# Four edits in one: fold transfers on GpSimd's queue and later in the MLP, transposes of memory values moved behind later work, and the two arms of a branch swapped with a branch hint

## The chip, the cores and the metric

One Trainium2 chip, one of its cores. The kernel is one launch; the time is the device time of that launch in microseconds (us). The kernel before was timed in three runs: 2238.1 us median, 2234.99 to 2240.84.

The engines of a core: TensorE (PE in the profile; PEld are its weight loads, which overlap the matmuls), VectorE (DVE), ScalarE (ACT), GpSimd (POOL) and SyncE (SP). SP computes nothing here; it issues most of the DMA transfers, in the order of its instruction queue. An instruction that waits for a semaphore holds everything behind it on its own engine's queue.

## The reference

One inference step of a two-layer decoder in fp32: width 1024, a prompt of 1024 tokens and 8 decode tokens that go along as 8 extra columns, feed-forward width 4096. Cut to what matters here:

```python
mk, mv = [], []
for l in range(2):
    k, v = split(rmsnorm(mem, norm_mem[l]) @ w_mem_kv[l], 2)      # 256 memory tokens, 4 heads of 64
    mk.append(k); mv.append(v)                                    # both are outputs, too
for l in range(2):
    if l == 1:                                                    # shared keys and values of the B layer
        ks, vs = split(rmsnorm(x, norm_kv) @ w_kv, 2)
    h = rmsnorm(x, norm_mix_pre[l])
    if l == 0:
        q, k, v, r, glr, qm = split(h @ w_in_a[0])                # 384, 384, 768, 768, 16, 256 columns
        g = log_sigmoid(glr @ w_gate_up + b_gate) / 16            # decay gates, per token and key column
        o_main = rmsnorm(gla_recurrence(q, k, v, g)) * silu(r)    # 4 heads, chunk-wise
    else:
        q, qm = split(h @ w_in_b[0])                              # 768, 256 columns
        o_main = sliding_window_attention(q, ks, vs)              # window 128, 12 heads, sinks
    o_mem = softmax(qm @ mk[l].T / 8) @ mv[l]                     # cross-attention into the memory
    x = x + rmsnorm(concat(o_main, o_mem) @ w_out[l])
    x = x + rmsnorm(square(relu(rmsnorm(x) @ w_ffn_up[l])) @ w_ffn_down[l])
```

The norm's gain is part of every `rmsnorm`. The chunk-wise recurrence needs the exponential of sums of gates over a block of 128 tokens, and its inverse. Where all gates are small enough both fit into fp32 at once; where not, the block must be cut into levels.

## The kernel before

**Layout.** Activations lie with the 1024 features over 8 groups of 128 partitions and the tokens along the free dimension, in three chunks of 384, 384 and 264 columns. Every fp32 product is made of three matmuls: operands are cut into a high part (an ACT cast, L152) and a rest (a DVE subtraction, L153), and `proj` (L244 to L246) adds high x high, high x rest and rest x high. Weights come as 128x1024 tiles of 512 KB, which `wload` brings in over SP's queue and cuts.

**Order.** The program is written in Python in one order; a planner reorders the instructions of each engine by priority (program order, unless `high_priority` lifts it) and by its own costs and then fixes one queue for each engine. An instruction can so stand in a queue well before or behind its place in the program, and matmuls of later projections fill the waits of attention.

**Stages of layer 0.** (1) Load of x, its norm and the projections of `qm`. (2) `memkv` (L1063): for both layers four units of 128 columns of the memory keys (m = 0, 1) and values (m = 2, 3), alternating with the projections of q and k (`qk_units`). Each unit is a `proj`, then a DVE multiplication by the norm into `kv` (L1073), one of two places in the tile `vtok`, then stores. For a value unit two PE transposes of `kv` follow (L1081), a DVE copy of them (L1082) and, after the last unit of a layer, a store of both units to DRAM (`mvd`, L1087), from where `load_memkv` reads them back. `gate_inputs` (L1168) then multiplies the gates' low-rank inputs by the norm (L1171, L1172, DVE) and sets a row of ones (L1173, L1174, GpSimd); its last piece lies where `memkv` had its transposed values. (3) `mem_attend_prompt` (L374): eight rounds (four pairs of token blocks, two pairs of heads), each a chain of scores (L384, PE), maximum (L389, DVE), exponentials (L392, ACT), division (L396, DVE), transposes (L403, PE), copy (L405, ACT), product with the values (L411, PE) and copy; with it go the `gates` (L1291) and the rest of the q and k projections. Then the attention of the decode tokens (`mem_dec_steps`, L423), and a reduction of all gates to one flag (L1335). (4) Every engine loads the flag into a register (L1463) and branches on it (L1465). The first arm, for small gates, does `one_factor` per block with the projections of v between; the second does the projections and then `by_levels`. With these inputs the first arm runs. In the program's memory the second arm lies behind it, and the first ends with a jump over it. (5) The recurrence (`gla_block`), the output projection, the MLP.

**The MLP** (`mlp`, L610) multiplies most of the hidden width by a Strassen-Winograd scheme: seven products of half-size blocks in place of eight. Its second half runs 49 *phases* (L927 on): seven products (`ORDER` = 1, 7, 6, 5, 2, 3, 4), each of seven steps jj. A phase is 48 matmuls (L910 to L912) into eight PSUM banks, which are emptied at the end of each product by `evict` (L571 to L585, DVE): product 1 by copies, product 6 (phases 14 to 20) with two additions per bank (L577, L578). For each phase, `load_a` brings 516 KB of activations from DRAM (`ra`, L863), `load_w` for four of the products 512 KB of weights (`wr`, L869), both over SP, and `prep` (L873) combines and cuts them on ACT and DVE (L152, L153, L879 to L887). `ra` has three buffers, and loads stand three phases ahead.

**The fold.** During layer 0's phases the twelve weight tiles of layer 1's projections (four of `w_kv`, eight of `w_in_b`) are multiplied by their norms' gains and written to a DRAM buffer `wfd`, from which layer 1 loads them (L1612). `fold(i)` is three instructions around one buffer `wf`: a load (L236, SP), a multiplication (L237, GpSimd) and a store (L238, SP). Fold i stands behind phase 3i + 2. The buffer's pool is closed behind phase 48, and its memory then belongs to the tiles of the MLP's result, written by L980.

Of the kernel before, what the change touches and what calls it, by code (L numbers as in the profile page):

```python
# [16 lines left out]
P = 128  # L17
# [6 lines left out]
NB = SEQ // P  # L24
MEM = 256
# [22 lines left out]
def hybrid_decoder_step(ctx: ExitStack, tc: tile.TileContext, A, O):  # L48
    nc = tc.nc
# [18 lines left out]
    ident = cp.tile([P, P], F32, tag="ident", name="ident")  # L68
# [21 lines left out]
    def nm(s):  # L90
        uid[0] += 1
        return f"{s}_{uid[0]}"
# [35 lines left out]
    def stps(tag=None):  # L128
        turn[1] ^= 1
        tag = tag or ("sf", "sx")[turn[1]]  # L130
        return pst.tile([P, 512], F32, tag=tag, name=nm(tag))
# [88 lines left out]
    def wstage(src, pool=None):  # L220
        with tc.high_priority(WPRI):
            ws = (pool or wp).tile([P, KT, P], F32, tag="ws", name=nm("ws"))
            nc.sync.dma_start(ws, src)
            return ws
# [8 lines left out]
    def fold(i, pool):  # L233
        src, g = (A["w_kv"][i], G_KV) if i < 4 else (A["w_in_b"][i - 4], G_MIXPRE + 1)
        ws = pool.tile([P, KT, P], F32, tag="wf", name=nm("wf"))
        nc.sync.dma_start(ws, src)  # L236
        nc.gpsimd.tensor_tensor(ws, ws, gains[:, g, :].unsqueeze(2).to_broadcast([P, KT, P]), ALU.mult)  # L237
        nc.sync.dma_start(wfd[i], ws)  # L238

    def proj(ps, w, hl, n, M=P, fine=False):  # L240
        wh, wl = w
# [129 lines left out]
                v = v.rearrange("p (a b c) -> p a b c", a=shape[1], b=shape[2])  # L371
            return v[: shape[0]]

    def mem_attend_prompt(ap, q, kt, vt, psS, psT, psO):  # L374
        for i2 in range(NB // 2):
            for hp in range(2):
                p = ap.tile([P, 2, 2, MEM], F32, tag="z", name=nm("p"))
                ps = psS().rearrange("p (j a b) -> p j a b", j=2, a=2)
                row = Row()
                for u in range(2):  # L380
                    i = 2 * i2 + u
                    for j in range(2):
                        rows = slice(64 * j, 64 * j + 64)
                        row(nc.tensor.matmul(ps[:, j, u, :], q[rows, hp, i * P : (i + 1) * P], kt[rows, hp, :],  # L384
                                             start=True, stop=True))
                sm = small(4, P, "msum")
                mx = small(4, P, "mx")
                ps3 = ps.rearrange("p j a b -> p (j a) b")
                nc.vector.tensor_reduce(mx, ps3, AX.X, ALU.max, negate=True)  # L389
                p3 = p.rearrange("p j u k -> p (j u) k")  # L390
                for o in range(4):
                    nc.scalar.activation(p3[:, o, :], ps3[:, o, :], AF.Exp, bias=mx[:, o : o + 1],  # L392
                                         accum_out=sm[:, o : o + 1])
                rs = small(4, P, "mrs")
                nc.vector.reciprocal(rs, sm)
                TT(p3, p3, rs.unsqueeze(2).to_broadcast([P, 4, MEM]), ALU.mult)  # L396
                row = Row()
                tps = psT()
                for j in range(2):
                    for mt in range(2):  # L400
                        for u in range(2):
                            o = (4 * j + 2 * mt + u) * P
                            row(nc.tensor.transpose(tps[:, o : o + P], p[:, j, u, mt * P : (mt + 1) * P], ident))  # L403
                pt = ap.tile([P, 2, 2, 2 * P], F32, tag="pt", name=nm("pt"), bufs=2)
                nc.scalar.copy(pt.rearrange("p j a b -> p (j a b)"), tps)  # L405
                po = psO()
                row = Row()
                for mt in range(2):
                    for j in range(2):
                        h = 2 * hp + j  # L410
                        row(nc.tensor.matmul(  # L411
                            po[64 * j : 64 * j + 64, : 2 * P], vt[:, mt, 64 * h : 64 * h + 64],
                            pt[:, j, mt, :], start=(mt == 0), stop=(mt == 1)))
                nc.scalar.copy(q[:, hp, i2 * 2 * P : (i2 + 1) * 2 * P], po[:, : 2 * P])
# [195 lines left out]
    def mlp(l, X, ff):  # L610
# [312 lines left out]
        with tc.high_priority(100):  # L923
            prep(0)
            prep(1)
        N = len(phases)
        for t in range(N):  # L927
            for u in ([3, 4, 5] if t == 0 else [t + 5]):
                if u < N:
                    load_w(u)  # L930
            if t + 3 < N:
                load_a(t + 3)
            if t + 2 < N:
                prep(t + 2)
            if t == N - 1:
                break
            phase(t)
            if l == 0 and t % 3 == 2 and t // 3 < 12:
                fold(t // 3, wfp)

        C = lambda m, h: acc[((11, 12), (21, 22))[m // 4][h]][:, m % 4]
        W = plain_weights(lambda m: A["w_down"][l, m],
# [117 lines left out]
        nc.sync.dma_start(ident, A["ident"])  # L1060
        return hl, prepare, mr

    def memkv(room, hl, prepare, mr):  # L1063
        for l in range(2):
            vtok = room[:, KT * MEM : (KT + 2) * MEM].rearrange("p (a b) -> p a b", a=2)
            if l:
                hl = prepare(1)
            for m in range(4):
                w = wload(wA, A["w_mem"][l, m])
                ps = mmps()  # L1070
                proj(ps, w, hl, MEM)
                kv = room[:, (KT + 2 + m % 2) * MEM : (KT + 3 + m % 2) * MEM]
                TT(kv, ps[:, :MEM], mr, ALU.mult)  # L1073
                if m < 2:
                    nc.sync.dma_start(O["mem_k"][l, :, m, :], kv)
                    nc.sync.dma_start(mkd[l, :, m, :], kv)
                else:
                    nc.sync.dma_start(O["mem_v"][l, :, m - 2, :], kv)
                    tps = stps()
                    for mt in range(2):  # L1080
                        nc.tensor.transpose(tps[:, mt * P : mt * P + P], kv[:, mt * P : mt * P + P], ident)  # L1081
                    nc.vector.tensor_copy(  # L1082
                        vtok[:, :, (m - 2) * P : (m - 1) * P],
                        tps[:, :MEM].rearrange("p (a b) -> p a b", a=2),
                    )
                    if m == 3:
                        nc.sync.dma_start(mvd[l], vtok)  # L1087
                yield

    def load_memkv(ap, l, room=None):  # L1090
        if room is None:
# [13 lines left out]
    with ExitStack() as sl0:  # L1105
# [10 lines left out]
        with ExitStack() as sla:  # L1116
# [152 lines left out]
            with tc.tile_pool(name="pm0", bufs=3, space=PSUM, reuse_waits="tile") as pm0:  # L1269
                set_extra(pm0, 3)  # L1270
                w0 = []
                gate_weights()
                load_x(lambda: w0.append(wload(wA, A["w_in_a"][18], 4 * WPRI)), gate_sums)
                with tc.tile_pool(name="memkv", bufs=1, reuse_waits="tile") as mp:
                    in_qm(0, w0[0], True)
                    room = vtok.rearrange("p a b -> p (a b)")
                    mem = memload(mp, room)
                    in_qm(1)
                    other = memkv(room, *mem)
                    for m in range(2):  # L1280
                        for c, _ in enumerate(qk_units(m)):
                            if m or c:
                                next(other)
                    for _ in other:
                        pass
                    gate_inputs()
                set_extra(None, 0)
            wg = vtok[:GR, 1:3, :192]
            nc.sync.dma_start(wg, A["wg"])
# [11 lines left out]
            with tc.tile_pool(name="pma0", bufs=1, space=PSUM, reuse_waits="tile") as pg:  # L1301
# [2 lines left out]
                psO = lambda: stps("sf")  # L1304
                with tc.tile_pool(name="ma0", bufs=2, reuse_waits="tile") as ap:
                    kt, vt = load_memkv(ap, 0, [vtok[:, i : i + 2, :MEM] for i in (4, 6)])
                    mem_attend_prompt(ap, qm, kt, vt, psS, psT, psO)
                for i in range(NB):
                    gates(i)
                gd = view(tp.tile([P, 768], F32, tag="t3", name="gd"), [NDEC, 2, 384])  # L1310
# [30 lines left out]
            with ExitStack() as sg:  # L1341
# [118 lines left out]
                nc.vector.tensor_copy(qd[:DK], qk[:DK, :, SEQ:NT])  # L1460
                W = [wload(wA, A["w_in_a"][6 + m]) for m in range(3)]
                staged = [wstage(A["w_in_a"][12 + m]) for m in range(2)] + [wstage(A["w_in_a"][6 + 3], g1)]
                small_range = nc.values_load(flag[0:1, 0:1], min_val=0, max_val=1)  # L1463
                with tc.tile_pool(name="gla", bufs=1, reuse_waits="tile") as gp:
                    with tc.If(small_range > 0) as cmp:  # L1465
                        parts = {0: one_factor(gp, 0)}

                        def ahead(u):
                            if u + 1 < NB:
                                parts[u + 1] = one_factor(gp, u + 1)  # L1470

                        def rest(u):
                            parts.pop(u)()

                        in_v(range(3), W, before=ahead, after=rest, part=slice(0, NB))()
                    with cmp.Else():
                        in_v(range(3), W, part=slice(0, NB))()
                        for i in range(NB):
                            by_levels(gp, i)

                pend = in_v(range(3), W, part=slice(NB, None))

# [486 lines left out]
```

## Time and profile before

| | us |
|---|---|
| median of three timed runs | 2238.1 |
| the profiled execution's own time | 2243.39 |
| its span, first to last instruction | 2241.6 |
| PE busy | 2165.5 (97%) |
| DVE busy | 1505.1 (67%) |
| ACT busy | 1060.2 (47%) |
| GpSimd busy | 90.0 (4%) |
| mean granted PE clock | 0.987 |

The profile shows one execution. Busy times are sums over an engine's instructions; the matmuls are pipelined, so a gap of PE is time in which none was under way. "Granted clock" is the share of full speed that PE's throttle allowed. A view of waits puts each idle time of an engine down to what ended it. A view by windows gives busy times between two moments of the span. The chain of waits goes back from the last instruction through what released each step. "issue" is a time in which nothing that the profile shows was waited for. PEld rows with a `q` (PEldq) are instructions of PE's sequencer.

### The profile page before, as it was taken

How to read it: one execution, taken by the hardware profiler on the slowest of the kernel's cores; microseconds unless marked ns; L12 is line 12 of the kernel's file. 1: busy time of each engine (PE TensorE's matmuls, PEld its weight loads, DVE VectorE, ACT ScalarE, POOL GpSimd, SP SyncE). 2: the span in 40 equal slices, each digit the busy share in tenths (PEclk: the TensorE clock that was granted, in tenths of full speed). 3: DMA queues.
4: the chain of work that ended last, by engine and by line, in shares of the span. 5: the costliest groups of instructions: out<-in, count | busy, mean ns of one | idle time of the engine just before them, and what ended most of it. 6: DMA issues, size and time to landing. Idle time of an engine off the chain costs nothing.

```text
span 2241.6 us, 40146 instructions
## 1 busy us (share of the span) xinstructions
PE 2165.5 (97%) x16250; PEld 2062.8 (92%) x16250; DVE 1505.1 (67%) x2811; ACT 1060.2 (47%) x2071; POOL 90.0 (4%) x99
## 2 busy tenths in 40 slices
PE   7999999899999999989999999899999999999997
PEld 5879897899999999989999878589999999999996
DVE  6656546758877776757469455646887777856557
ACT  6354435547654444333324355555765445433333
POOL 0002000000000000320000000200000000000010
PEclk9999999999999999999999999999999999999998
DMA  5512026434544448574325200414263446635422
GB/s 183 163 62 73 21 64 154 151 96 135 167 157 157 156 145 329 197 268 138 100 74 151 94 20 21 123 62 141 92 224 128 156 157 225 242 114 162 152 89 76
DMA packets 134691, 303.72 MB, mean 135 GB/s; under 512 B 11033, under 2 KB 65489, under 8 KB 134209
## 3 DMA queue, kind: packets, MB, share of 16 engines
q1 hardware_dynamic: 120192, 271.39, 36.7%
q0 software_dynamic: 4368, 16.85, 2.3%
q10 hardware_dynamic: 9936, 12.81, 1.6%
q8 instruction: 130, 2.13, 0.4%
q14 instruction: 65, 0.53, 0.1%
HBM read 213.57 MB, written 89.51 MB: 135 GB/s over the span
## 4 chain that ended last, share of the span: by engine, by line
PE 77%; DMA 6%; DVE 5%; ACT 2%; POOL 1%; issue 1%; SPq 0%; DVEq 0%; ACTq 0%; POOLq 0%
PE mm L244 5%; PE mx L745 5%; PE mx L746 5%; PE mm L246 5%; PE mx L747 5%; PE mm L245 5%; PE mx L910 3%; PE mx L912 3%; PE mx L911 3%; PE mm L745 2%; PE mm L746 2%; PE mm L747 2%; PE mx L244 2%; PE mx L246 2%; PE mx L245 2%; PE mm L910 2%
## 5 line engine op out<-in xcount | busy, mean ns | idle before, releaser
L152 ACT CAST wh<-ws 128x512 fp32r<-128x512 f32 (+1 forms) x262 | 188.1, 725 | 323.9 <-DVE ws L598 103.8
L153 DVE TENSOR_TENSOR wl<-ws,wh 128x512 fp32r<-128x512 f32 (+1 forms) x262 | 213.4, 821 | 133.7 <-ACT wh L152 133.1
L745 PE MATMUL mx<-xf,wh 128*128 128x258 f32 x1048 | 297.7, 284 | 0.0
L746 PE MATMUL mx<-xf,wh 128*128 128x258 f32 x1048 | 296.0, 282 | 0.0
L747 PE MATMUL mx<-xf,wl 128*128 128x258 f32 x1048 | 295.1, 282 | 0.0
L244 PE MATMUL mm<-xh,wh 128*128 128x384 f32 (+1 forms) x864 | 282.4, 327 | 3.3 <-issue 2.6
L246 PE MATMUL mm<-xh,wl 128*128 128x384 f32 (+1 forms) x864 | 280.6, 325 | 2.1 <-issue 2.1
L245 PE MATMUL mm<-xl,wh 128*128 128x384 f32 (+1 forms) x864 | 278.5, 322 | 0.0
L152 ACT CAST wh<-wr 128x1024 fp32r<-128x1024 f32 x98 | 102.9, 1050 | 293.1 <-PE sx L911 274.8
L910 PE MATMUL mx<-sa,wh 128*128 128x258 f32 x784 | 222.3, 284 | 8.0 <-DVE acc L578 5.7
L153 DVE TENSOR_TENSOR wl<-wr,wh 128x1024 fp32r<-128x1024 f32 x98 | 121.5, 1240 | 150.4 <-ACT wh L152 150.3
L911 PE MATMUL mx<-sa,wh 128*128 128x258 f32 x784 | 221.3, 282 | 0.3 <-DVE sa L153 0.3
L912 PE MATMUL mx<-sa,wl 128*128 128x258 f32 x784 | 221.0, 282 | 0.0
L746 PEld LDWEIGHTS mx<-xf,wh 128*128 128x128 f32 x1048 | 198.0, 189 | 0.4
L745 PEld LDWEIGHTS mx<-xf,wh 128*128 128x128 f32 x1048 | 197.6, 189 | 0.4
L747 PEld LDWEIGHTS mx<-xf,wl 128*128 128x128 f32 x1048 | 197.9, 189 | 0.0
L244 PEld LDWEIGHTS mm<-xh,wh 128*128 128x128 f32 x864 | 163.8, 190 | 14.5 <-issue 10.7
L246 PEld LDWEIGHTS mm<-xh,wl 128*128 128x128 f32 x864 | 163.5, 189 | 9.6 <-issue 7.7
L245 PEld LDWEIGHTS mm<-xl,wh 128*128 128x128 f32 x864 | 163.9, 190 | 5.0 <-issue 3.8
L910 PEld LDWEIGHTS mx<-sa,wh 128*128 128x128 f32 x784 | 148.1, 189 | 8.9 <-issue 5.9
L911 PEld LDWEIGHTS mx<-sa,wh 128*128 128x128 f32 x784 | 149.0, 190 | 0.5 <-DVE sa L153 0.5
L153 DVE TENSOR_TENSOR sa<-ra,sa 128x1032 fp32r<-128x1032 f32 x98 | 125.7, 1282 | 35.1 <-ACT sa L152 35.1
(543 smaller groups left out, 5768.4 us busy)
## 6 DMA issues: line engine op xcount, KB each, us to landing
ra<-awd SPq DMA_DIRECT2D x98, 516.0 KB, 4.3
ws<-in_w_up SPq DMA_DIRECT2D x64, 512.0 KB, 6.5
wr<-in_w_downb SPq DMA_DIRECT2D x56, 512.0 KB, 5.6
awd<-aw SPq DMA_DIRECT2D x26, 1032.0 KB, 6.8
awd<-am SPq DMA_DIRECT2D x28, 774.0 KB, 8.4
ws<-in_w_in_a SPq DMA_DIRECT2D x20, 512.0 KB, 3.7
xd<-f ACTq DMA_DIRECT2D x24, 384.0 KB, 4.7
ws<-in_w_out SPq DMA_DIRECT2D x16, 512.0 KB, 3.6
```

Source lines behind the costliest of these rows:

```text
L152: nc.scalar.copy(hi, src)
L153: (eng or nc.vector).tensor_tensor(lo, src, f32(hi), ALU.subtract)
L244: nc.tensor.matmul(ps[:M, :n], wh[:, k, :M], xh[:, k, :], start=(k == 0), stop=False)
L245: nc.tensor.matmul(ps[:M, :n], wh[:, k, :M], xl[:, k, :], start=False, stop=False)
L246: mm = nc.tensor.matmul(ps[:M, :n], wl[:, k, :M], xh[:, k, :], start=False, stop=(k == KT - 1))
L745: nc.tensor.matmul(ps, wh(k), xh, start=(k == 0), stop=False)
L746: nc.tensor.matmul(ps, wh(k), xl, start=False, stop=False)
L747: mm = nc.tensor.matmul(ps, wl(k), xh, start=False, stop=(k == n - 1))
L910: nc.tensor.matmul(ps, wh[:, q, ms], h, start=(jj == 0 and q == 0), stop=False)
L911: nc.tensor.matmul(ps, wh[:, q, ms], lo, start=False, stop=False)
L912: mm = nc.tensor.matmul(ps, wl[:, q, ms], h, start=False, stop=end)
```

## The change

1. **Fold.** The load and the store of `fold` are issued by GpSimd (the software queue) in place of SP. The twelve folds stand behind the phases 21, 23, 25, 27, 35, 36, 38, 40, 41, 43, 45 and 46, in the order in which layer 1 uses the tiles, in place of phases 2, 5, ..., 35.
2. **Memory values.** The two transposes of a value unit, their copy and the store to `mvd` are put off until the `proj` of the next unit has been issued. The last one (layer 1, m = 3) is handed to the attention, which issues it ahead of its third round.
3. **Gate inputs.** `gate_inputs` moves from in front of the attention to behind that last transposition, also ahead of the third round.
4. **Branch.** The condition is turned round and the arms are swapped: `by_levels` is now the first arm, and the arm that runs with these inputs is `Else`. Ahead of the load of the flag, PE, ACT and DVE get a branch hint that the branch is likely taken.

```diff
     def fold(i, pool):
         ws = pool.tile([P, KT, P], F32, tag="wf", name=nm("wf"))
-        nc.sync.dma_start(ws, src)
+        nc.gpsimd.dma_start(ws, src)
         nc.gpsimd.tensor_tensor(ws, ws, gains[:, g, :].unsqueeze(2).to_broadcast([P, KT, P]), ALU.mult)
-        nc.sync.dma_start(wfd[i], ws)
+        nc.gpsimd.dma_start(wfd[i], ws)
...
-    def mem_attend_prompt(ap, q, kt, vt, psS, psT, psO):
+    def mem_attend_prompt(ap, q, kt, vt, psS, psT, psO, between=None):
         for i2 in range(NB // 2):
             for hp in range(2):
+                if between and (i2, hp) == (1, 0):
+                    between()
...
+        folds = dict(zip((21, 23, 25, 27, 35, 36, 38, 40, 41, 43, 45, 46), (2, 3, 0, 1, 10, 11, 4, 5, 6, 7, 8, 9)))
         for t in range(N):
...
             phase(t)
-            if l == 0 and t % 3 == 2 and t // 3 < 12:
-                fold(t // 3, wfp)
+            if l == 0 and t in folds:
+                fold(folds.pop(t), wfp)
...
-    def memkv(room, hl, prepare, mr):
+    def memkv(left, room, hl, prepare, mr):
+        pend = None
         for l in range(2):
...
                 proj(ps, w, hl, MEM)
+                if pend:
+                    pend()
+                    pend = None
                 kv = room[:, (KT + 2 + m % 2) * MEM : (KT + 3 + m % 2) * MEM]
                 TT(kv, ps[:, :MEM], mr, ALU.mult)
...
                     nc.sync.dma_start(O["mem_v"][l, :, m - 2, :], kv)
-                    tps = stps()
...
+
+                    def pend(l=l, m=m, kv=kv, vtok=vtok):
+                        tps = stps()
+                        for mt in range(2):
+                            nc.tensor.transpose(tps[:, mt * P : mt * P + P], kv[:, mt * P : mt * P + P], ident)
+                        nc.vector.tensor_copy(
+                            vtok[:, :, (m - 2) * P : (m - 1) * P],
+                            tps[:, :MEM].rearrange("p (a b) -> p a b", a=2),
+                        )
+                        if m == 3:
+                            nc.sync.dma_start(mvd[l], vtok)
                 yield
+        left.append(pend)
...
-                    gate_inputs()
...
-                    mem_attend_prompt(ap, qm, kt, vt, psS, psT, psO)
+
+                    def between():
+                        left.pop()()
+                        gate_inputs()
+
+                    mem_attend_prompt(ap, qm, kt, vt, psS, psT, psO, between)
...
+                tc.mark_branch_hint_location(
+                    "gates", "LikelyTaken", (mybir.EngineType.PE, mybir.EngineType.Activation, mybir.EngineType.DVE))
                 small_range = nc.values_load(flag[0:1, 0:1], min_val=0, max_val=1)
                 with tc.tile_pool(name="gla", bufs=1, reuse_waits="tile") as gp:
-                    with tc.If(small_range > 0) as cmp:
+                    with tc.If(small_range < 1, label="gates") as cmp:
+                        in_v(range(3), W, part=slice(0, NB))()
+                        for i in range(NB):
+                            by_levels(gp, i)
+                    with cmp.Else():
                         parts = {0: one_factor(gp, 0)}
...
                         in_v(range(3), W, before=ahead, after=rest, part=slice(0, NB))()
-                    with cmp.Else():
-                        in_v(range(3), W, part=slice(0, NB))()
-                        for i in range(NB):
-                            by_levels(gp, i)
```

More of the change, by code (lines that the diff above doesn't have):

```diff
@@ L1078, in memkv @@
                     nc.sync.dma_start(O["mem_v"][l, :, m - 2, :], kv)
-                    tps = stps()
[L1080 to L1087, printed above, removed]
+                    def pend(l=l, m=m, kv=kv, vtok=vtok):
[8 more added lines that the diff above has]
+                            nc.sync.dma_start(mvd[l], vtok)
                 yield
+        left.append(pend)
     def load_memkv(ap, l, room=None):
@@ L1278, in hybrid_decoder_step @@
                     in_qm(1)
-                    other = memkv(room, *mem)
+                    left = []
+                    other = memkv(left, room, *mem)
                     for m in range(2):
```

## The prediction

> **What bounds the kernel now.** I read the page first, for which engine sets the end, then the waits of that engine by stage.
>
> ```profile
> span 2241.6 us, 40146 instructions
> PE 2165.5 (97%) x16250; PEld 2062.8 (92%) x16250; DVE 1505.1 (67%) x2811; ACT 1060.2 (47%) x2071; POOL 90.0 (4%) x99
> ```
>
> PE is busy for 97% of the span, so an edit that removes no PE work can win only what PE stands idle, and what it loses to a lower clock just after. Three stages that the change touches have such gaps. For the MLP's second half I set four windows of layer 0 (phases 0 to 12, 13, 14 to 19, 20 and 21) beside the same phases of layer 1, which has no folds.
>
> ```profile
> core 0: us, PE busy (x) PEld busy (x) DVE busy (x) ACT busy (x) POOL busy (x), PEclk, DMA share, GB/s
> 849.40:925.30 75.90, 75.16 (x626) 74.78 (x625) 60.12 (x52) 32.17 (x39) 13.34 (x5) 1.00 0.82 302
> 925.30:933.20 7.90, 6.30 (x51) 5.91 (x49) 7.90 (x9) 3.05 (x3) 7.90 (x1) 1.00 0.00 1
> 933.20:967.80 34.60, 34.60 (x289) 34.60 (x290) 17.15 (x18) 10.13 (x10) 8.79 (x4) 1.00 0.54 186
> 967.80:986.70 18.90, 13.20 (x99) 13.02 (x98) 11.22 (x21) 5.06 (x5) 3.80 (x2) 0.82 0.73 264
> 1893.10:1968.40 75.30, 75.04 (x626) 74.83 (x625) 57.81 (x54) 31.32 (x38) 0.00 (x0) 1.00 0.70 248
> 1968.40:1974.20 5.80, 5.80 (x50) 5.80 (x49) 4.63 (x9) 2.00 (x2) 0.00 (x0) 1.00 0.31 96
> 1974.20:2008.70 34.50, 34.50 (x290) 34.50 (x289) 14.85 (x14) 12.03 (x12) 0.00 (x0) 1.00 0.31 104
> 2008.70:2020.20 11.50, 11.50 (x99) 11.50 (x98) 9.98 (x20) 4.01 (x4) 0.00 (x0) 1.00 0.39 129
> ```
>
> Layer 0 takes 137.3 us for 22 phases, layer 1 takes 127.1: 10.2 us more. Nearly all lies in the second and fourth pair: 7.90 against 5.80, and 18.90 against 11.50. In the second the DMA engines of layer 0 move 1 GB/s, nothing. The chain of waits says why:
>
> ```profile
> 915.17 7.39 DMA wf<-in_w_in_b
> 922.68 11.78 POOL wf L237
> ...
> 966.36 3.39 DMA wf<-in_w_in_b
> 969.91 1.91 POOL wf L237
> 971.84 0.32 SPq L238
> 972.25 3.89 DMA ra<-awd
> 976.24 1.06 ACT sa L152
> 977.32 1.23 DVE sa L153
> ```
>
> SP waits in order for the fold's multiplication (L238 <- L237), and the activations' load `ra` stands behind it; its cut on DVE at 977.32 then holds the evictions that PE needs. The waits of SP's queue (855 to 1005 us) and of PE (845 to 1142 us) give the totals:
>
> ```profile
> SPq L238 <- POOL wf L237: 80.9, 12, 14.5
> SPq L236 <- DMA wfd<-wf: 17.7, 11, 2.6
> ...
> PE mx L910 <- DVE acc L578: 5.7, 1, 5.7
> PE mx L910 <- DVE acc L575: 1.3, 1, 1.3
> ```
>
> **The fold: -9.0 us.** SP loses 24 issues and 98.6 us (80.9 + 17.7) of waiting out of 150. Of the 10.2 us, 7.0 are PE's two gaps (5.7 + 1.3); most of the rest is the clock (0.82 in the window of the large gap). The 0.6 of the first pair (75.90 against 75.30) begin ahead of the first fold, so 9.6 can be won, and 0 if the late loads had another cause. I take 9.0: layer 1 is this stage without folds and has no such gap, and I leave 0.6 for collisions with GpSimd's transfers. GpSimd gets two issues per fold and the waiting. What it then queues up is only the next fold. Its transfers:
>
> ```profile
> L237 POOL TENSOR_TENSOR wf<-wf,gains x12: 1898/2618/11768, 869.2 to 997.5; 128x1024 f32<-128x1024 f32 x12
> xall<-xd POOLq DMA_DIRECT2D x8, 384.0 KB, 5.9
> L214 SPq DMA_DIRECT2D ws<-wfd x12: 319/329/333, 1132.8 to 1284.2; - x12
> L980 DVE TENSOR_TENSOR f<-mm,acc x11: 550/551/558, 1144.8 to 2208.7; 128x384 f32<-128x384 f32 x11
> ```
>
> Now a fold takes (997.5 - 869.2) / 11 = 11.7 us. Through GpSimd's queue I estimate 5.9 + 2.6 + 5.9 = 14.4 us, from the 384 KB load there and the median multiplication. Nothing else stands in that queue, so the new places alone should not hold the folds; twelve from 869 end at 869 + 12 x 14.4 = 1042, ahead of the first read of `wfd` at 1132.8 and of the first write into the reused memory (at the earliest 1144.8). That slack, 90 us or more, is the cover; a later end would cost PE its whole overrun.
>
> A rule speaks against this part. The Trainium skill, page "DMA: Bandwidth & Descriptors", section "Issuing engines are not separate DMA queues", says that issuing from several engines saves only the sequencer's time, "which is usually small relative to the DMA itself". By it the sum would lose its 9.0; but the trace disagrees where it shows SP held 80.9 us by another engine's work, not by issuing.
>
> **Memory values and gate inputs: -5.1 us.** PE's and DVE's waits from 70 to 104 us, and the clock behind the second gap:
>
> ```profile
> PE sx L1081 <- DVE vtok L1073: 2.7, 2, 2.4
> PE sf L1081 <- DVE vtok L1073: 2.4, 1, 2.4
> ...
> DVE vtok L1073 <- DMA mkd<-vtok: 2.1, 1, 2.1
> ...
> 101.90:105.40 3.50, 3.04 (x9) 2.44 (x10) 3.00 (x4) 1.25 (x3) 0.00 (x0) 0.51 0.59 177
> ```
>
> No instruction goes. DVE's L1073 still waits 2.1 us for a store, but PE has a whole `proj` in its queue ahead of the transposes, so 2.7 + 2.4 = 5.1 us of gaps are filled, and of 3.04 us at clock 0.51 about half, 1.5: together 6.6. The nine DVE steps and two memsets of the gate inputs cost nothing on PE (attention's chain is filled by projections); if DVE were held by the store ahead of L1172, that chain would slip by one such wait, 2.1. What is late next is the branch's flag: attention starts only about 2.7 us earlier (the first gap and its small companion), while PE's fill work ends 6.6 earlier. I charge 1.5 for that (below), so 5.1; ends 0 to 6.6, and -2 (a loss) if the planner's new order leaves DVE waiting.
>
> **The branch: -6.0 us.** PE's waits from 240 to 260 us, the window behind them, and the branch's own rows:
>
> ```profile
> PE mm L244 <- issue: 2.6, 1, 2.6
> PE mm L246 <- issue: 2.1, 1, 2.1
> ...
> 248.70:255.60 6.90, 5.72 (x24) 5.72 (x25) 3.03 (x4) 1.56 (x4) 0.00 (x0) 0.51 0.48 152
> ...
> L1465 PEldq COMPARE_BRANCH x2: 92/1730/3368, 188.9 to 243.1; - x2
> L1465 POOLq COMPARE_BRANCH x2: 41/42/44, 186.7 to 234.9; - x2
> L1335 DVE CAST flag<-sm x1: 134/134/134, 185.9 to 185.9; 1x1 int32<-1x1 f32 x1
> 190.44 1.04 PE L1367 MATMUL gL<-triu_c,vtok 128*96 128x128 f32 x8
> 246.91 1.99 ACT L152 CAST wh<-ws 128x1024 fp32r<-128x1024 f32 x2 [2.50 <-issue]
> ```
>
> Falling into the first arm costs PE 92 ns, the jump over the second 3368. Nothing is awaited then but instructions: 2.6 us at the jump's target and 2.1 a little behind it. With the clock at 0.51 for 5.72 us of work (about half lost, less for short matmuls: 2.6, an estimate), the exit costs 7.3. Afterwards the arm that runs is last and falls through, so these go. In their place stands a jump at the entry. With a hint that works it costs PE about as little as the entry does now, 92 ns. Without one it costs the same 3.37 us from 188.9, ending at 192.3; PE's queue still holds matmuls until 190.44, so 1.9 us show, and with luck as bad as at the exit 2.1 + 2.6 more. So the gain lies between 0.7 and 7.3; I take 6.0, as the hint's lead is unknown. DVE and ACT jump, too: ACT idles 2.5 us for it now. At the entry PE's first gate sums and projection cover this on both; bare, it would be 2.5 once. GpSimd gets no hint, but branches at 186.7, so that 3.4 us more still end ahead of PE's first matmul of the arm, 190.44.
>
> A rule speaks against this part as well: the Trainium skill, "Runtime: NRT & Kernel Launch", section "Instruction fetch mechanics", says that a taken branch whose target is not in the window already fetched stalls for the fetch. By it alone the stall only moves to the entry, and the sum would be 2 to 5 us less; no run here shows a hint.
>
> The flag lands at 186.1 and PE's branch comes at 188.9: 2.8 us of slack, which falls to 2.8 - (6.6 - 2.7) = -1.1. PE's queue covers 1.5 (190.44 - 188.9), but not a jump as well; hence the 1.5 charged.
>
> **Sum.** 9.0 + 5.1 + 6.0 = 20.1. Against the profiled execution: span 2241.6 - 20.1 = 2221.5, its own time 2243.39 - 20.1 = 2223.3. That execution lies 5.3 above the median of the runs, 2238.1; from the median, **2218 us**.
>
> **The rivals.**
>
> *The folds were not the cause.* The loads are late because 0.82 of the DMA engines' time is taken from 849 to 925 us, and they stay late, with the folds' transfers at the same engines. For it: 302 GB/s. Against it: layer 1 runs at 0.70 with no gap, and the DMA engines stand still just ahead of the first gap. Time: 2238.1 - 5.1 - 6.0 = 2227. The Trainium skill's rule on issuing engines, named above, gives the same.
>
> *The hint does nothing, or the flag is late.* The entry pays 1.9 + 4.7, so the third part gives 7.3 - 6.6 = 0.7; with the cover spent on that, the second gives only what attention starts earlier, 2.7. For it: the slack of -1.1 and an instruction that was never timed here. Against it: 92 ns at the entry now, and no fetch as unlucky as the exit's second is due there. 9.0 + 2.7 + 0.7 = 12.4: 2226.
>
> *Slower: the fold's chain ends too late.* Place: phases 42 to 48 and the memory handed to L980. If the folds do start only at their new places (phase 21, which now begins behind the large gap at about 979; 970 after the gains) they must take less than (1144.8 - 970) / 12 = 14.6 us each. The slowest multiplication, 11.8 us, came while DVE was busy for all of 7.90 us; the folds on which DVE leans so take 5.9 + 11.8 + 5.9 = 23.6. From 16.9 us a fold the loss outweighs the 20 us won and the 0.3% that a measurement can tell (14.6 + 27 / 12). At 20 us each they end at 1210, 65 late: 2218 + 65 = 2283. Against it: GpSimd's queue holds nothing that would delay the first fold, and in the late phases DVE is less busy.
>
> **How the numbers follow.** The forecast (the sum, each term within 3 us, 2211 to 2225): 0.65. The folds not the cause: 0.10. Hint or flag: 0.15. Slower: 0.05. The remaining 0.05 is a new order of the planner that gives back what was won, about 2238. The range goes from 2210 (all three upper ends, 9.6 + 6.6 + 7.3 = 23.5, give 2214.6; the rest is for smaller half-clock stretches that close) to 2232 (both rivals at 2226 and 2227 with 5 us of their own scatter for half-clock stretches that open elsewhere); it leaves out the last two cases and the tails. 0.3% is 6.7 us, so faster means under 2231.4: 0.84, the first three cases less 0.06 of tails. Within 0.3%: 0.10. Slower by more: 0.06.
>
> **What would show it.** Phases 0 to 21 of layer 0 take about 128 us, with `ra` no longer behind `wf` in the chain and no stretch of 1 GB/s. PE has no wait for L1073, and no half clock near 102. The 3368 ns branch is gone, the entry's is short, and PE's wait for "issue" at 244 vanishes. Wrong would be: PE waiting at L910 for L578 as before; PE idle ahead of L1367; a fold's store beyond 1132; or a wait for `wfd` in layer 1.

## The result and the profile after

The changed kernel takes 2226.4 us in the median (2223.5 to 2228.8, six runs) against 2239.9 for the kernel before, timed beside it (2235.0 to 2244.9, six runs): 13.6 us less, a ratio of 0.9939 with a 95% interval of 0.9926 to 0.9952. The profiled executions lie further apart: 2224.17 after, 2243.39 before, 19.2 less. The page of the kernel after:

```profile
span 2222.4 us, 40138 instructions
PE 2161.7 (97%) x16250; PEld 2059.6 (93%) x16250; DVE 1503.2 (68%) x2811; ACT 1061.5 (48%) x2071; POOL 115.4 (5%) x123
```

Every kernel's rows carry its own line numbers. In the kernel after, the attention's scores are L386, its exponentials L394, the division L398, the transposes L405, the load of `ra` L865, a phase L912 to L914, the flag L1350, the branch L1482.

*MLP.* The same four windows by phases (0 to 12, 13, 14 to 19, 20 and 21) of the kernel after:

```profile
841.10:915.90 74.80, 74.80 (x627) 74.80 (x626) 59.95 (x52) 29.97 (x37) 34.50 (x12) 1.00 0.81 294
915.90:921.70 5.80, 5.80 (x51) 5.80 (x50) 4.66 (x9) 2.00 (x2) 1.07 (x2) 1.00 0.57 199
921.70:953.40 31.70, 31.70 (x268) 31.70 (x267) 16.02 (x14) 12.04 (x12) 10.50 (x8) 1.00 0.55 191
953.40:967.60 14.20, 14.20 (x121) 14.20 (x120) 10.48 (x21) 4.01 (x4) 3.55 (x4) 1.00 0.67 231
```

PE is busy in all of 126.5 us, where it was 137.3; the half clock is gone, too. PE's waits from 835 to 1125 us have no row left. The folds, by the rows of the tile `wf` and the buffer `wfd` (first and last start behind the durations):

```profile
L237 POOL TENSOR_TENSOR wf<-wf,gains x12: 1894/2468/24447, 850.0 to 1007.8; 128x1024 f32<-128x1024 f32 x12
L238 POOL DMA_DIRECT2D wfd<-wf x12: 599/599/602, 852.5 to 1010.7; - x12
L214 SPq DMA_DIRECT2D ws<-wfd x12: 319/329/333, 1113.8 to 1265.3; - x12
```

SP's largest entry of waits from 845 to 1015 us:

```profile
SPq L865 <- DVE sa L153: 95.3, 27, 7.2
```

SP now waits for a buffer of `ra` to come free (L865), that is, it runs ahead of need instead of behind GpSimd. Twelve folds start 14.3 us apart, (1007.8 - 850.0) / 11, and the last store is issued 103 us ahead of the first read of `wfd`.

*Attention.* PE's waits from 40 to 192 us of the kernel after, all rows; before, this view had 2.7 + 2.4 for L1081 and 2.2 of others:

```profile
PE sT L405 <- DVE p L398: 2.1, 5, 0.7
PE sA L386 <- ACT p L394: 1.5, 1, 1.5
PE sx L1304 <- issue: 0.7, 1, 0.7
```

The transposes wait no more, but the chain of the attention does: 4.3 us against 7.3. So in this pair 3.0 of the 5.1 us of gaps are kept.

*Branch.* The flag's line, then its load by PE and the branch of PE:

```profile
L1350 DVE CAST flag<-sm x1: 134/134/134, 183.9 to 183.9; 1x1 int32<-1x1 f32 x1
```

```profile
L1480 PEldq TENSOR_LOAD <-flag x1: 489/489/489, 186.3 to 186.3; - x1
```

```profile
L1482 PEldq COMPARE_BRANCH  x1: 481/481/481, 186.9 to 186.9; - x1
```

The flag is written at 184.04, and PE loads it at 186.26, 2.2 us later. The jump costs PE 481 ns, there is one branch in place of two, and PE has no wait of 0.3 us or more from 185 to 260 us.

Between the traces the gain builds up so: the arm's first matmul comes 2.0 us earlier, the decode tokens' stage behind the arm 9.1, the first phase 8.3, phase 13 9.5, phase 22 19.0, the end 19.2.

### The profile page after: what moved, and what is told of

The parts are those of the page before. It is cut to its first block, busy times and chain, and to the rows that moved or that the text cites. A ratio compares the mean times of both kernels' runs of the same rounds, so it can differ in the third digit from the quotient of the medians.

```text
span 2222.4 us, 40138 instructions
## 1 busy us (share of the span) xinstructions
PE 2161.7 (97%) x16250; PEld 2059.6 (93%) x16250; DVE 1503.2 (68%) x2811; ACT 1061.5 (48%) x2071; POOL 115.4 (5%) x123
## 4 chain that ended last, share of the span: by engine, by line
PE 91%; DVE 4%; ACT 2%; DMA 1%; issue 1%; SPq 0%; DVEq 0%; ACTq 0%
PE mx L747 6%; PE mm L244 6%; PE mx L748 6%; PE mx L749 6%; PE mm L246 6%; PE mm L245 6%; PE mx L912 4%; PE mx L914 4%; PE mx L913 4%; PE mx L244 3%; PE mx L246 3%; PE mx L245 3%; PE mm L747 3%; PE mm L748 3%; PE mm L749 3%; PE mm L912 2%
## 5 line engine op out<-in xcount | busy, mean ns | idle before, releaser
L244 PE MATMUL mm<-xh,wh 128*128 128x384 f32 (+1 forms) x864 | 281.5, 326 | 0.7 <-ACT xh L152 0.5
L246 PE MATMUL mm<-xh,wl 128*128 128x384 f32 (+1 forms) x864 | 279.0, 323 | 0.0
L912 PE MATMUL mx<-sa,wh 128*128 128x258 f32 x784 | 221.3, 283 | 0.0
L914 PE MATMUL mx<-sa,wl 128*128 128x258 f32 x784 | 220.4, 281 | 0.0
L244 PEld LDWEIGHTS mm<-xh,wh 128*128 128x128 f32 x864 | 163.0, 189 | 10.6 <-issue 6.7
L246 PEld LDWEIGHTS mm<-xh,wl 128*128 128x128 f32 x864 | 162.7, 188 | 7.3 <-issue 5.2
L913 PEld LDWEIGHTS mx<-sa,wh 128*128 128x128 f32 x784 | 148.3, 189 | 0.0
L914 PEld LDWEIGHTS mx<-sa,wl 128*128 128x128 f32 x784 | 148.0, 189 | 0.0
L747 PE MATMUL mm<-xf,wh 128*128 128x258 f32 x520 | 147.6, 284 | 0.0
```

Of the source, the lines that this page charges most:

```text
L244: nc.tensor.matmul(ps[:M, :n], wh[:, k, :M], xh[:, k, :], start=(k == 0), stop=False)
L246: mm = nc.tensor.matmul(ps[:M, :n], wl[:, k, :M], xh[:, k, :], start=False, stop=(k == KT - 1))
L747: nc.tensor.matmul(ps, wh(k), xh, start=(k == 0), stop=False)
L912: nc.tensor.matmul(ps, wh[:, q, ms], h, start=(jj == 0 and q == 0), stop=False)
L913: nc.tensor.matmul(ps, wh[:, q, ms], lo, start=False, stop=False)
L914: mm = nc.tensor.matmul(ps, wl[:, q, ms], h, start=False, stop=end)
```

## The experiments

Theory: the three mechanisms are those of the prediction, but the gaps of one execution are not those of the median; above all the fold's loss differs from execution to execution. Rival: one part gives nothing, and another more than its share. The first four kernels make one part each.

**The folds alone.** The code cuts of this section show the lines that matter.

```diff
-        nc.sync.dma_start(ws, src)                  # the store too
+        nc.gpsimd.dma_start(ws, src)
-            if l == 0 and t % 3 == 2 and t // 3 < 12:
+            if l == 0 and t in folds:               # 21, 23, ..., 46
```

> The kernel before with the fold's edit alone (load and store by GpSimd, new places). In the one pair of traces the phases 0 to 21 became 10.7 us shorter, while the timed medians of the whole change differ by 13.6 against 19.2 between the two profiled executions. Theory A, the profiled execution of before was one of its longer ones, and it is the fold's two gaps of PE that vary from run to run: the median falls by 4 to 6 us, and in this trace phases 0 to 21 take 126 to 128 us. Theory B, the gaps are the same in each run and the shortfall lies in another part: the median falls by 9 to 11 us. Rival, the DMA engines and not SP's queue made the loads late: no fall.

Measured: 2234.1 us against 2240.0, ratio 0.9975 (0.9962 to 0.9988); the means differ by 5.4. Phases 13 to 21 take 51.8 us at full clock, as they do after the whole change. Phases 0 to 12 take 76.5 in this trace, so phases 0 to 21 come to 128.3, just above the 126 to 128 of theory A.

**Memory values and gate inputs alone** (the diff's parts 2 and 3).

```diff
+        left.append(pend)
-                    gate_inputs()
+                    def between():
+                        left.pop()()
+                        gate_inputs()
```

> The kernel before with the put-off transposes and the later gate inputs alone. Prediction: 5.1 us less. From the traces: PE reaches the arm behind the branch 2.0 us earlier than before (188.4 against 190.4), of which 0.7 was lost ahead of 58 us already, so 2 to 3 us less. Rival, it is worth nothing, since the attention's rounds and not PE's waits for the transposes set the time of the flag: 0 to 1 us less, with PE idle ahead of the scores of the second round.

Measured: 2236.7 us, ratio 0.9983 (0.9966 to 1.0); the means differ by 2.5. In its trace the arm starts 1.7 us earlier than in the first trace of the kernel before (188.8 against 190.4). That alone shows nothing: a second trace of the unchanged kernel, reported below, starts it at 188.3. This trace also shows the folds' trouble in another shape. PE's wait at the start of phase 13:

```profile
PE mx L913 <- DVE sa L153: 5.5, 1, 5.5
```

And the window behind it, at clock 0.50:

```profile
925.70:932.50 6.80, 5.13 (x24) 5.13 (x25) 6.80 (x7) 0.00 (x0) 0.33 (x1) 0.50 0.50 177
```

**The branch alone, with and without the hint.**

```diff
+                tc.mark_branch_hint_location("gates", "LikelyTaken", ...)   # not in the second kernel
-                    with tc.If(small_range > 0) as cmp:
+                    with tc.If(small_range < 1, label="gates") as cmp:
```

> The kernel before with the arms swapped and the hint alone. Prediction: 6.0 us less, 7.3 if the hint hides the whole fetch. From the traces: 7.1 us between the arm's first and the decode stage's first matmul. So 6 to 7.5 us less; PE's branch at the entry takes about 0.5 us and PE does not idle ahead of L1367's matmuls. Rival, half of the 7.1 us are the clock's half-speed windows, which fall differently from run to run: 4 to 5 us less.

> The arms swapped without the hint. Theory, the hint hides the fetch: here PE's branch at the entry takes 3.4 us, PE idles 1.9 us ahead of the arm's first matmul, and with a second fetch up to 2.1 us more, so the median falls by 2 to 5 us only, 2 to 5 us behind the version with the hint. Rival, the hint does nothing and the order of the arms does all: the same time as the version with the hint.

Measured with the hint: 2233.1 us, ratio 0.9970 (0.9953 to 0.9986), means 6.0 apart. Without it: 2240.3 us, ratio 0.9999 (0.9983 to 1.0015), means 0.9 apart. PE's branch with the hint, and without it:

```profile
L1467 PEldq COMPARE_BRANCH  x1: 726/726/726, 188.4 to 188.4; - x1
```

```profile
L1465 PEldq COMPARE_BRANCH  x1: 3523/3523/3523, 188.2 to 188.2; - x1
```

PE's longest wait without the hint, from 180 to 260 us:

```profile
PE gL L1367 <- DVE qd L1460: 2.1, 1, 2.1
```

The wait is put down to DVE, but the branch ends at 191.7, 188.2 + 3.5, and the gap just behind it, at 192.0. Yet the trace of the bare swap looked good: only those 2.1 us at the entry, the exit's gaps and its half clock gone, so 5 us should have been won where the median won nothing. Theory: in other executions the gap at the entry brings on a half clock.

> The swapped arms without the hint, one more trace. Theory: the 2.1 us idle before the arm's first matmul brings on a half-clock window in some executions; a trace of such an execution shows PE at half clock between 185 and 200 us and the arm's start another 1 to 3 us later. Rival: the trace is like the first (gap of 2.1 us, full clock, exit gap gone), the decode stage starts 5 to 6 us earlier than in the kernel before, and the equal median stays unexplained by the entry.

> The swapped arms without the hint, timed again on the chip of this call. If its unchanged median was an accident of which executions were drawn, it now comes out 3 to 6 us below the kernel before, as its two traces have it (the exit's stalls and half clock gone, 2.1 to 2.4 us of idle at the entry instead). If the hint is what the gain hangs on, the median is again within 2 us of the kernel before; a trace of an execution above 2238 us then shows where: theory, a half-clock window between 185 and 205 us; rival, none there, and the lost time is spread over other stages.

The second trace was like the first (gap 2.4 us, full clock, 2232.4 us). The new timing gave 2234.8 against 2236.6, ratio 0.9991 (0.9977 to 1.0005), means 1.0 apart, and its profile fell on an execution of 2240 us of span, which shows the theory's window. PE's branch in it:

```profile
L1465 PEldq COMPARE_BRANCH  x1: 4063/4063/4063, 188.8 to 188.8; - x1
```

PE's wait from 180 to 215 us:

```profile
PE gL L1367 <- DVE wl L153: 2.6, 1, 2.6
```

The window behind it:

```profile
192.60:202.80 10.20, 9.64 (x44) 9.67 (x45) 4.24 (x9) 5.45 (x18) 2.07 (x3) 0.50 0.17 57
```

10.2 us at half clock. The arm takes 45.9 us from its first gate sum to its last, 41.3 in the two other traces: 4.6 more. With the 2.6 of the gap that is 7.2, as much as the exit cost before (7.3 in the trace of the branch alone). From the means, 7.3 - 1.0 = 6.3, an execution without the hint pays mostly the dear form; that is a conclusion from the times, since only three executions were seen.

**What the folds cost, and which half of the edit matters.**

```diff
# the queue alone
-        nc.sync.dma_start(ws, src)
+        nc.gpsimd.dma_start(ws, src)
# the places alone
-            if l == 0 and t % 3 == 2 and t // 3 < 12:
+            if l == 0 and t in folds:
# no folds
-                W = [wload(..., wfd[j]) ...]
+                W = [wload(..., A["w_kv"][j] if j < 4 else A["w_in_b"][j - 4]) ...]
```

> The kernel before with the folds issued by GpSimd at their old places. Theory, the queue does all and the place nothing, since nothing in GpSimd's queue holds a fold back (in the traces with the new places the first multiplication starts at 850 to 854 us, not at phase 21): 5.4 us less than before like the whole fold edit, and the multiplications start at the same times as there. Rival, the place counts: a time between, 1 to 3 us less.

> The folds at the new places, but still over SP's queue. Theory, SP waits for GpSimd wherever the folds stand; from phase 21 on DVE has more room and no product with two evictions per bank is left, so the multiplications are not starved and the loads less late: half of the 5.4 us, 2 to 4 us less, with SP's wait for the multiplication at 30 to 60 us in place of 80.9. Rival, the waiting only moves to later phases: no change. If it alone gives all 5.4, the queue was not needed.

> No folds at all: layer 1 loads its weights as they are, so its gains are left out of the computation. This bounds what the fold costs in the kernel before. Theory A (its cost differs from run to run, 3 to 9.6 us in the five traces that have it): 5 to 7 us less, a spread of the times under 3 us as with the fold's edit, against 4.3 before, and phases 13 to 21 take 51.5 to 52 us. Theory B (it costs 9.6 each time): 9 to 10 us less.

> The kernel before once more, for another trace of it. Phases 13 to 21 took 61.2 us in the first trace, 59.9, 56.3 and 54.7 in three versions that left the folds alone, and 51.7 with the fold's edit. Theory A: another time between 54 and 61, with PE's two gaps of another size. Theory B: 61 again.

| | median, us | ratio, 95% interval | phases 13 to 21, us |
|---|---|---|---|
| before (29 runs beside the three) | 2235.8 | 1 | 55.2 |
| queue alone | 2232.2 | 0.9985, 0.9975 to 0.9996 | 51.7 |
| places alone | 2233.1 | 0.9984, 0.9972 to 0.9997 | 53.1 |
| no folds | 2231.6 | 0.9982, 0.9969 to 0.9995 | 51.7 |

By the means the three gain 3.7, 3.7 and 4.0 us, and their intervals overlap: on this chip either half of the edit does what leaving the folds out does. The queue alone was expected to give 5.4 or 1 to 3 and came out between; no folds were expected to give 5 to 7 and came out below. Without any fold the kernel gains 4.2 us in the median, so the term could never be 9.0 there. The second trace of the kernel before explains it: SP waits 71.7 us for the folds' multiplications (850 to 1005 us) where it was 80.9, but PE only 1.7 + 1.3 around them (845 to 1142 us), with no half clock:

```profile
SPq L238 <- POOL wf L237: 71.7, 12, 8.4
```

```profile
PE mx L911 <- DVE sa L153: 1.7, 1, 1.7
PE mx L910 <- DVE acc L575: 1.3, 1, 1.3
```

Seven traces have the folds over SP at the old places. Their phases 13 to 21 take 61.2, 59.9, 59.3, 56.3, 55.2, 54.7 and 54.0 us, against 51.7 without folds: between 2.3 and 9.5 more, 5.5 in the mean and 4.6 in the median. The profile that the prediction read was the longest of them. The three long ones have a gap of over 5 us with a half clock behind it, the four others neither.

What sets the three apart is one multiplication of GpSimd. The longest of the twelve took 11.8, 10.2 and 13.4 us in the three long traces, and 3.7 to 4.2 in the four short ones. The second trace of the kernel before is one of these:

```profile
L237 POOL TENSOR_TENSOR wf<-wf,gains x12: 1899/2515/4061, 868.3 to 988.6; 128x1024 f32<-128x1024 f32 x12
```

SP's longest single wait for it is 12.0 to 14.5 us in the three, 7.9 to 8.4 in the four. In two of the three (the first trace of the kernel before and the third of the bare swap) the loads `ra` of phases 17, 19, 21 and 22 then land only 0.1 us before their cast; in the four short traces they land 2.5 to 6.5 us before it. In the third (memory part alone) a load of weights stands behind the held store, and DVE waits 9.1 us for it. So it is the long wait that uses up the lead of the loads, not the sum of the waits. The folds' edit also narrows the times: the standard deviation falls from 3.6 to 1.1 us with the queue alone.

The places alone do as well by the median, although SP still waits nearly as long (850 to 1020 us):

```profile
SPq L238 <- POOL wf L237: 65.8, 12, 8.2
...
SPq L236 <- DMA wfd<-wf: 22.2, 11, 2.4
```

The first row was expected at 30 to 60 us. So SP's waiting as such is not the cost. These folds start at 900 instead of 869 us and stand behind other loads. The first multiplication is long here, too, 9.2 us; but the `ra` loads of phases 8 to 13 landed 8.4 to 10.5 us ahead of use, against 4.3 to 8.0 in the first trace of the kernel before, and SP's longest wait is 8.2. In this trace the folds cost 1.4 us in phases 13 to 21 (53.1 against 51.7). A gap of 1.3 at 1013 comes later; one of the same length stands at 1001 in the second trace of the whole change, so it need not be SP's.

**The whole, and the whole without the memory part.**

```diff
# the second kernel: parts 1 and 4 only
-                    mem_attend_prompt(ap, qm, kt, vt, psS, psT, psO, between)
+                    gate_inputs()
+                    mem_attend_prompt(ap, qm, kt, vt, psS, psT, psO)
```

> The whole change once more. If the three parts add up, as the single runs' means do (-5.4 for the folds, -2.5 for memory values and gate inputs, -6.0 for the branch), it is 11 to 14 us below the kernel before on this chip. If the first profiled pair showed the true size, it is 19 to 20 us below. In its trace: a taken branch under 0.8 us and no half-clock window within 5 us of the exit from layer 0's arm by either.

> Folds and branch changed, memory values and gate inputs left as in the kernel before. If the memory part brings its 2.5 us in the combination too, this stands 8 to 11 us below the kernel before and 2 to 3 us above the whole change of the same call. If the new waits in the attention take back what the part saves, it is equal to the whole change within 1 us.

Measured, the whole: 2224.9 us against 2238.2, ratio 0.9939 (0.9922 to 0.9956); without the memory part 2227.2, ratio 0.9945 (0.9925 to 0.9964). The means lie 13.6 and 11.4 below. The single parts, 5.4 + 2.5 + 6.0, make 13.9: they add up. In the trace of the whole PE's branch takes 486 ns and no half clock lies near the exit, as expected. The memory part's 2.3 us in the median lie within both intervals, so the times alone don't settle it; the trace without it shows what it removes. PE's waits from 70 to 112 us:

```profile
PE sx L1082 <- DVE vtok L1074: 3.6, 1, 3.6
PE sf L1082 <- DVE vtok L1074: 2.0, 1, 2.0
```

The window behind the first:

```profile
75.80:82.60 6.80, 5.24 (x17) 5.24 (x18) 3.02 (x6) 0.54 (x1) 0.00 (x0) 0.50 0.65 211
```

No kernel here is faster than the whole change.

## Why the prediction was right, and where it was not

**The sum.** The prediction subtracted 20.1 from one profiled execution and got 2223.3; the profiled execution after took 2224.17. It then put the same 20.1 against the median of other executions, 2218, and there 13.6 came. That step failed: the prediction itself noted that its execution lay 5.3 above the median, and did not ask whether the gaps it was about to remove were what made it longer. To a large part they were. Nor did the 0.65 case hold as it was drawn, 2211 to 2225: the measured 2226.4 lies above it, inside the whole range alone. That 2223.3 met 2224.17 is partly luck; a second profiled execution of the same kernel took 2220.28.

**The fold, 9.0.** The cause was right: a store held by GpSimd's multiplication makes the loads behind it late. In the pair of traces phases 13 to 21 lose 9.5 us (61.2 to 51.7) and phases 0 to 12 another 1.1. The term was mis-sized for the median: 5.4 by the means with the edit, 4.0 without any fold. Layer 1 as "this stage without folds" was the right yardstick for the end state, 126.5 us here, but it measured one execution's excess, one of the three of seven with a multiplication above 10 us. The chain of waits showed that very one, 11.78 us, among eleven others of 1.9 to 2.9. The queue's half was not needed for the gain: the places alone gave as much. The estimate of 14.4 us a fold met 14.3, but by terms that offset each other: the load 5.4 in place of 5.9, the multiplication 4.2 in the mean in place of 2.6, the store 3.5 in place of 5.9, and 1.1 for issuing the two. The folds did not wait for phase 21; they started at 850.0, as the prediction's cover needed, and the slower rival's condition (a start at 970 and over 16.9 us each) never came about. Its slow multiplication did: 24.4 us once, with no wait of PE.

The rival "the folds were not the cause" named 2227, and 2226.4 was measured. It is false all the same: phases 13 to 21 are cured in every kernel with the queue changed, and the folds alone win 5.4 us. The rival of the useless hint or the late flag named 2226 and is false, too: the jump took 481 ns, and the flag kept its lead. A time near a rival's is no proof of it. On the rule that it leaned on, that issuing from several engines saves only the sequencer's time (the Trainium skill, "DMA: Bandwidth & Descriptors", section "Issuing engines are not separate DMA queues"): the queue alone gave 0.9985, so as a forecast of no gain it fails here; not the time to issue was saved, but the waiting ahead of the loads.

**Memory values and gate inputs, 5.1.** By the means it is 2.5 alone and 2.2 in the combination. The gaps for L1081 went, as said. What failed is the step that PE's queue would overtake the flag, at 1.5. Its slack, counted as there from the flag (184.04) to PE's branch (186.86), is 2.8 us as before, where -1.1 was forecast; in all fourteen traces PE loads the flag 2.2 us after it is written, so the two moved together. Instead the attention's own matmuls wait for ACT and DVE, 1.5 for L394 and 2.1 in place of 1.3 for the division; "the attention's chain is filled by projections" was too much. That this is because the fill work is spent earlier or because DVE does the gate inputs between was not separated. The half clock behind the second gap, counted at 1.5, is also no fixed sum: of the eleven traces with the old order, seven have it.

The fourteen traces tell what the part is worth. From one and the same projection matmul (the 201st of L244 to L246, at 57 to 59 us) to PE's branch the old order took 129.0 to 133.4 us, 130.5 in the mean, the three traces with the new order 128.2 to 128.6, 128.3 in the mean: 2.2 less, as the times have it. The three old traces without any half clock in this stretch took 129.0, 129.4 and 129.5. So without the clock the part is worth 1.0 us: from that matmul to the arm's first PE idles 2.1 us less than in these three, but is busy for 1.2 more, and why was not shown. The other half of the gain is half clock, which eight of the eleven old traces have there and none of the three new ones.

**The branch, 6.0.** 6.0 by the means, 7.1 to 7.3 in the traces beside the first one of the kernel before. From the arm's first matmul to one well behind the exit the seven traces of the old branch order take 6.2 to 7.5 us more than the kernel after, so the size was right. The hint's lead was the unknown; the four traces with the hint have 481, 486, 726 and 826 ns, and none has a wait of PE above 0.2 us from 180 to 260 us. The lower bound, 0.7 with a hint that does nothing, is what the bare swap gives, 0.9 and 1.0. The rule that the stall only moves to the entry (the Trainium skill, "Runtime: NRT & Kernel Launch", section "Instruction fetch mechanics") holds for the swap without the hint, 3.5 to 4.1 us, and not with it.

## What to carry to other kernels

A profile is one execution: before its gaps are subtracted from a median, look whether that execution is longer than the median and whether those very gaps make it so; a second trace of the kernel before would have shown 55.2 us where the first had 61.2. A sum of waits in an in-order queue says little of its price: 85 to 99 us of SP's cost 2 to 10 us in seven traces. What decided was the longest single wait beside the lead of the loads behind it, and whether one instruction among twelve like ones is an outlier. The same work without the edit, or left out, gives the price. A branch whose usual arm lies far off wants a hint; swapping the arms alone only moves the stall.

## What the runs showed of the hardware

**The clock decides what a gap costs.** Up to the last 20 us of a trace, stretches of half clock last 3.4 us or a multiple (6.8, 10.2, 13.7). Single gaps of 1.8 to 2.7 us bring them, and not always: the bare swap's gap had none after 2.1 and 2.4 us and 10.2 us of it after 2.6. The two gaps at the exit had a stretch of 6.8 in all seven traces of the old branch order, and none of the seven traces with swapped arms has one there. At the second memory transposes the seven traces with 2.0 us or more idle have one, the four with 1.5 to 1.9 have none; at the first, 2.3 to 2.6 us bring one in two traces of nine, and 3.5 and 3.6 us brought one in each of the other two. The Trainium skill, "TensorE: Matmul & The Clock Gate", section "What's actually happening", has a free-running window of about 3.4 us, which fits the lengths and the luck; the section "HAM oscillation — how this bites in real kernels" warns only of idle gaps above about 3.4 us, and these runs show the loss from shorter ones.

The spread between executions is mostly this clock. Of eleven executions of the kernel before on one chip the shortest, 2228.7 us, had a mean granted clock of 0.991, the longest, 2243.7, of 0.984: 0.007 x 2240 = 15.7 us of lost clock, beside 15.0 of difference.

**A GpSimd multiplication can be starved.** The one of 24.4 us in the kernel after lies in this window:

```profile
891.10:915.60 24.50, 24.50 (x207) 24.50 (x206) 22.68 (x20) 8.02 (x8) 24.44 (x1) 1.00 0.49 154
```

DVE is busy for 22.7 of 24.5 us, with subtractions and sums of two operands. The usual multiplication takes 1.9 to 2.9 us. With the folds over SP the longest of a trace took 3.7 to 13.4, with GpSimd's queue 14.2 to 24.4; there it cost PE no wait, since only the next fold stood behind it.

Nine multiplications in the fourteen traces took over 9 us. Each ran beside an unbroken row of DVE instructions with two operands in SBUF, and each ended 1.76 us after the last of these, that is, about one usual multiplication later. In the first trace of the kernel before, GpSimd's instruction:

```profile
922.68 11.77 POOL L237 TENSOR_TENSOR wf<-wf,gains 128x1024 f32<-128x1024 f32 x1 [10.42 <-DMA wf<-in_w_in_b]
```

and the end of DVE's row:

```profile
931.47 1.22 DVE L153 TENSOR_TENSOR sa<-ra,sa 128x1032 fp32r<-128x1032 f32 x1
932.62 1.41 DVE L575 TENSOR_TENSOR acc<-mx,acc 128x258 f32<-128x258 f32 x4
```

It ends at 934.45, while DVE already runs the evictions of L575, which take one operand from PSUM: these did not hold it. In the kernel after, DVE is idle from 913.8 and the multiplication ends at 915.5. The Trainium skill, "SBUF — State Buffer", section "SBUF: two separate sides", says that a DVE instruction with two SBUF inputs and a GpSimd instruction exclude each other from a shared port pair for a whole instruction. The traces agree with that, though no row of them shows the lock itself.
